# A mixture-of-experts layer on one core: the further block moved behind gate_up, the general test moved to expert 29

## The chip, the cores and the metric

The kernel runs on one core of a Trainium2 chip. The metric is the device time of one execution in microseconds (us), the median of several runs. A profiled execution has a span, from its first to its last instruction, and a little around it that counts in the time but not in the span.

## What is computed

One layer over 256 tokens of width 1024. A first part (modulated norm, four mixers, output projection) ends in a hidden state. Then every token goes to 4 of 32 experts, with softmax gates, and the result is added to the stream and normed:

```
def expert_block(args):
    xb, e = args
    gu = xb @ w_gu[e] + b_gu[e]
    gt = jnp.minimum(gu[:, :D_FF], SWIGLU_LIMIT)
    up = jnp.clip(gu[:, D_FF:], -SWIGLU_LIMIT, SWIGLU_LIMIT)
    act = (up + 1) * (gt * jax.nn.sigmoid(SWIGLU_ALPHA * gt))
    return act @ w_down[e] + b_down[e]
...
x = x + g2 * moe(h_x.reshape(-1, D), *moe_p).reshape(bn, L, D)
return rmsnorm(x, final_norm_g)
```

All weights are float32: 8 MB of gate/up and 4 MB of down weights for each expert, some 400 MB in all. Each is used once, unless an expert has more tokens than fit a block.

## The kernel before

The first part takes some 170 us; the rest is a loop over the experts, in an order written out by hand (each engine runs its instructions in the order of the program; waits between engines are set automatically, as counts of finished work of the engine waited for).

**The ring of weights.** `stream` lists the 192 loads: six for an expert, four of gate/up weights (u = 0 to 3, two of the eight k-slices each) and two of down weights (u = 4, 5), 2 MB each; at the end the last down half of expert 30 stands behind the gate/up loads of expert 31, and the very last load is cut in two. `load_unit(i, e, u)` (lines 566 to 584) puts load i into ring place i mod 9 (`NPAIR`) and notes in `wt` and `dn` where the products find it. `load_to(n)` issues all loads up to n, on SP's queue. Load i must wait until the last instruction that reads load i-9 is done. In the body of expert e, `load_to(e * NUN + NPAIR)` stands behind `down(e - 1)` and issues the loads whose places expert e-1 has used.

**An expert.** The tokens of expert e (the first 64, `CAP`) have been picked one step before. `gate_up(e, XET)` (line 964) multiplies them by the gate/up weights into two banks, four matmuls for each k-slice, so sixteen for each load as the trace counts them. Beside that run `pick` (the next expert's tokens), `swiglu` on VectorE and ScalarE, the transposes `turn_rows` and `turn_act`, and parts of the scatter of the pair of experts before (`adds`: one for an odd expert, three for an even one). `down(e, ...)` (line 992) is the second product; in the program it stands at the beginning of the next expert's body. `keep` moves its result out.

**Further blocks.** If expert e (0 to 29) has over 64 tokens, `block(e, CAP, ...)` (line 1033) computes 32 more with the same weights, both products of them. It is under `tc.If(r > CAP)` on TensorE, VectorE and ScalarE (line 1114), behind `down(e - 1)` and ahead of `gate_up(e)`. `r` is read from the table of counts (`CNT`). On the branch not taken each of these engines does one step that raises its count by what the block would have added.

**The general path** (lines 1149 to 1165) is for inputs in which an expert has still more tokens, or one of the last two over 64. It loads weights again, six loads for each expert, and runs as many blocks as are wanted. Its test is on these engines and SP, behind `gate_up(31)`, in the middle of `down(30)`: four k-slices of `down(30)` stand ahead of `gate_up(31)` and four behind the test. It is not taken for this input.

**The end.** Behind it stand the second half of `down(30)`, `turn_act(AT2)`, and the down product of expert 31 in pieces (`down_half`, line 1011), the last scatter (line 1026) and the final norm.

Of the kernel before, what the change touches and what calls it, by code (L numbers as in the profile page):

```python
# [11 lines left out]
ENG = mybir.EngineType  # L12
# [4 lines left out]
L = 256  # L17
KT = D // P
NE = 32
TOPK = 4  # L20
EPS = 1e-6
CAP = 64
MORE = 32
SLOT = 2048
NSLOT = 18
NUN = 6
NPAIR = NSLOT // 2
# [17 lines left out]

M0 = NSLOT * SLOT
O_ID, O_IOTA, O_POSM, O_GATE, O_VEC = M0, M0 + 128, M0 + 384, M0 + 448, M0 + 512
O_FGB, O_G2B, O_H = M0 + 768, M0 + 1792, M0 + 2304
O_XE, O_XET, O_P, O_PG, O_S = M0 + 4352, M0 + 4864, M0 + 5376, M0 + 5888, M0 + 6144
O_GH, O_TH, O_UP, O_AT, O_O = M0 + 6656, M0 + 7168, M0 + 7680, M0 + 8192, M0 + 8704  # L50
# [19 lines left out]
def tile_hybrid_moe(tc, x, ctx, vec, mats, const, pos_col, pos_row, rows, bias, w_mod, w_in, w_out,  # L70
                    w_gu, w_down, out):
    nc = tc.nc
    pe, dve, act, pool, sp = nc.tensor, nc.vector, nc.scalar, nc.gpsimd, nc.sync

    with tc.tile_pool(name="big", bufs=1) as big, tc.tile_pool(name="acc", bufs=1, space=PSUM) as acc_pool, \
# [7 lines left out]
        CNT = big.tile([1, NE + 1], I32, name="CNT")  # L83
        bank = [acc_pool.tile([P, 512], F32, name=f"bank{i}") for i in range(8)]

        def R(off, n):
            return B[:, off:off + n]

        def slot(i):
            return R(i * SLOT, SLOT)  # L90

# [14 lines left out]
        YT = slot(17).rearrange("p (k n) -> p k n", k=KT)  # L106
        UT = R(14 * SLOT, 4096).rearrange("p (k n) -> p k n", k=KT)
        W_1 = R(8 * SLOT, 8 * 768).rearrange("p (k n) -> p k n", k=KT)
        W_2 = R(11 * SLOT, 8 * 768).rearrange("p (k n) -> p k n", k=KT)
        BMR = R(O_BM, 2048)  # L110
# [357 lines left out]

        sets = [[R(i * SLOT + 512 * j, 512) for j in range(4)] for i in (4, 5, 6, 7)]
        order = [(0, 0), (1, 0), (0, 1), (1, 1)]  # L470
# [88 lines left out]
        wt, dn = {}, {}  # L559
# [3 lines left out]
        stream = [(e, u) for e in range(NE - 2) for u in range(NUN)]  # L563
        stream += [(NE - 2, u) for u in range(5)] + [(NE - 1, u) for u in range(4)] + [(NE - 2, 5), (NE - 1, 4), (NE - 1, 5)]

        def load_unit(i, e, u):

            s = R(2 * RING[i % NPAIR] * SLOT, 2 * SLOT)
            if u < 4:

                sp.dma_start(s, w_gu[e, 256 * u:256 * u + 256, :].rearrange("(p k) n -> p (k n)", k=2))
                for b in range(2):
                    wt[e, 2 * u + b] = s[:, 2048 * b:2048 * b + 2048]
            else:

                h = u - 4
                rows4 = w_down[e, 512 * h:512 * h + 512, :].rearrange("(p k) n -> p k n", k=4)

                step = 2 if (e, u) == (NE - 1, NUN - 1) else 4
                for b in range(0, 4, step):  # L580
                    sp.dma_start(s[:, 1024 * b:1024 * (b + step)].rearrange("p (k n) -> p k n", k=step), rows4[:, b:b + step, :])
                for b in range(4):
                    for q in range(2):
                        dn[e, 4 * h + b, q] = s[:, 1024 * b + 512 * q:1024 * b + 512 * q + 512]

        def load_to(n):
            while nxt[0] < min(n, NE * NUN):
                e, u = stream[nxt[0]]
                load_unit(nxt[0], e, u)
                nxt[0] += 1  # L590
# [307 lines left out]
        GH, TH, UP = R(O_GH, 512), R(O_TH, 512), R(O_UP, 512)  # L898
# [7 lines left out]
        G0, G1 = bank[4], bank[5]  # L906
        mis = [bank[0], bank[1]]
# [7 lines left out]
        def gated(pr):  # L915
            p = PP[pr % 2]
            e0 = 2 * pr
            dve.tensor_tensor(out=PGf.rearrange("p (c e s) -> p c e s", c=2, e=2), in0=p,
                              in1=GT[:, :, e0:e0 + 2].unsqueeze(3).to_broadcast([P, 2, 2, CAP]), op=ALU.mult)
# [40 lines left out]
        def bias_mm(dst, e, col, g):  # L960
            pe.matmul(dst[64 * g:64 * g + 64, :], E3[:, e:e + 1].to_broadcast([96, CAP]), T[:, col:col + 512],  # L961
                      start=True, stop=False)

        def gate_up(e, xt):
            for b, dst in enumerate((G0, G1)):
                for g in range(2):
                    bias_mm(dst, e, b * 1024 + g * 512, g)
            for k in range(KT):
                w = wt[e, k]
                for b, dst in enumerate((G0, G1)):  # L970
                    for g in range(2):
                        pe.matmul(dst[64 * g:64 * g + 64, :], xt[:, k % 4, (k // 4) * 64:(k // 4) * 64 + 64],  # L972
                                  w[:, b * 1024 + g * 512:b * 1024 + g * 512 + 512], start=False, stop=(k == KT - 1))
# [18 lines left out]
        def down(e, dst, ks=range(KT)):  # L992
            for g in range(2):
                if ks[0] == 0:
                    bias_mm(dst, e, 2048 + g * 512, g)
            for k in ks:
                for g in range(2):
                    pe.matmul(dst[64 * g:64 * g + 64, :], AT[:, k % 4, (k // 4) * 64:(k // 4) * 64 + 64],  # L998
                              dn[e, k, g], start=False, stop=(k == KT - 1))
# [20 lines left out]
        def keep(dst, p0, ps):  # L1020
            for g in range(2):
                dve.tensor_tensor(out=dst[p0:p0 + 64, 512 * g:512 * g + 512], in0=ps[64 * g:64 * g + 64, :],  # L1022
                                  in1=G2B[64 * g:64 * g + 64, :], op=ALU.mult)

        def scatter_part(s, o, c, q, a=0, b=512, last=False):
            pe.matmul(Y[c][q][:, a:b], s[:, c * P:(c + 1) * P], o[:, 512 * q + a:512 * q + b], start=False, stop=last)  # L1026
# [6 lines left out]
        def block(e, base, ga, gb, gh, th, up):  # L1033

            n = MORE
            quarter = [slice(n * g, n * g + n) for g in range(4)]
# [46 lines left out]
        engines = [ENG.PE, ENG.DVE, ENG.Activation]  # L1083
# [8 lines left out]
        dve.tensor_reduce(out=cl, in_=CN[0:1, NE - 2:NE], op=ALU.max, axis=mybir.AxisListType.X)  # L1092
        dve.tensor_scalar(cm, cl, float(MORE), cm, op0=ALU.add, op1=ALU.max)
        dve.tensor_copy(CNT[:, NE:NE + 1], cm)
# [6 lines left out]
        pool.memset(VPG, 0.0)  # L1101
        pool.memset(VO, 0.0)
        load_to(NPAIR)

        parts = [(0, 0), (0, 1), (1, 0), (1, 1)]
        for e in range(NE - 1):
            pr, par = divmod(e, 2)
            if e < NE - 2:
                r = nc.values_load(CNT[0:1, e:e + 1], min_val=0, max_val=L, engines=engines)
            if e > 0:  # L1110
                down(e - 1, mis[1])
                load_to(e * NUN + NPAIR)
            if e < NE - 2:
                with tc.If(r > CAP):  # L1114
                    block(e, CAP, G0, G1, GH, TH, UP)
            if e > 0:
                keep(OP[(e - 1) // 2 % 2], 64 * ((e - 1) % 2), mis[1])
            mine = parts if e == NE - 2 else parts[3:] if par else parts[:3]
            adds = [lambda c=c, q=q: scatter_part(SS[(pr - 1) % 2], OP[(pr - 1) % 2], c, q) for c, q in mine]
            adds = adds if pr > 0 else []  # L1120
            gate_up(e, XET)
            if e == NE - 2:
                load_to(NE * NUN)
            pick(PP[(e + 1) // 2 % 2][:, :, (e + 1) % 2, :])

            swiglu()
            picked()
            for f in adds[:1]:
                f()
            turn_rows(XET, mis[1])  # L1130
            turn_act(AT)
            for f in adds[1:]:
                f()
            if par == 1:
                s_pair(PGf, SS[(pr + 1) % 2], G1)
            elif e == 0:
                gated(0)
                s_pair(PGf, SS[0], G1)
            if par == 0 and e + 2 < NE:
                one_hot(pr + 1)  # L1140
                gated(pr + 1)
        e = NE - 1
        more = engines + [ENG.SP]
        r = nc.values_load(CNT[0:1, NE:NE + 1], min_val=0, max_val=L + MORE, engines=more)
        down(e - 1, mis[1], range(4))
        gate_up(e, XET)
        swiglu()

        with tc.If(r > CAP + MORE):  # L1149
            kept = dict(wt), dict(dn)  # L1150
            for e in range(NE):
                base = CAP if e >= NE - 2 else CAP + MORE
                r = nc.values_load(CNT[0:1, e:e + 1], min_val=0, max_val=L, engines=more)
                with tc.If(r > base):
                    for u in range(NUN):
                        load_unit(3 + u, e, u)
                    for b in range(base, L, MORE):
                        args = e, b, mis[0], mis[0], R(O_O, 512), R(O_O + 512, 512), R(O_XET, 512)
                        if b == base:
                            block(*args)  # L1160
                        else:
                            with tc.If(r > b):
                                block(*args)
            for now, old in zip((wt, dn), kept):
                now.update(old)
        e = NE - 1
        down(e - 1, mis[1], range(4, KT))
        keep(OP[1], 0, mis[1])
# [140 lines left out]
```

## Time and profile before

| | us |
|---|---|
| median of 3 runs | 1111.02 (1110.48 to 1111.2) |
| the profiled execution, its time | 1112.09 |
| its span | 1110.3 |
| TensorE (PE) busy | 1025.7 |
| VectorE (DVE) busy | 305.6 |
| ScalarE (ACT) busy | 128.5 |
| moved by the DMA queues | 445.59 MB, mean 401 GB/s |

The page's slices show the busy share of each engine in 40 equal parts of the span, in tenths; PEclk is the granted clock of TensorE in tenths of full speed; under them stand the mean busy share of the 16 DMA engines and the GB/s that they moved. In the timeline a row is a run of like instructions of one line: its start, how long it lasts, engine and line, what is written from what, how many, and in brackets the idle time ahead of it with what ended it. SPq is SP's queue, whose rows are issues of DMAs, PEld TensorE's weight loads, and a q behind an engine its sequencer.

### The profile page before, as it was taken

The page shows a single profiled execution, that of the slowest core. Times are in us where ns is not written, and L with a number is a line of the kernel's source. Part 1 is how long each engine was busy: PE and PEld are TensorE (multiplying, and loading weights), DVE is VectorE, ACT ScalarE, POOL GpSimd, SP SyncE. Part 2 cuts the span into 40 slices and gives each one's busy share as a digit, 9 for nine tenths or more (in the row PEclk, how much of TensorE's full clock was granted, in tenths as well). Part 3 has the DMA queues.
Part 4 walks back from the last instruction along what each step waited for, and adds up shares of the span by engine and source line. Part 5 has one row for each costly group of instructions (what it writes and reads, how often), then busy time and mean ns, then how long its engine had stood idle before and what let it go on. Part 6 is the DMA issues. An engine that isn't in the chain of part 4 may idle for free. (4 is left out here: it accounts for less than half of the span.)

```text
span 1110.3 us, 11952 instructions
## 1 busy us (share of the span) xinstructions
PE 1025.7 (92%) x4932; PEld 435.8 (39%) x4932; DVE 305.6 (28%) x593; ACT 128.5 (12%) x239; POOL 34.6 (3%) x77
## 2 busy tenths in 40 slices
PE   4999988999999989999999999999989898988896
PEld 2665865333333333333333333333333333323333
DVE  5488742121212222121212121212111212111113
ACT  4133430000000000000000000000000000000002
POOL 4102120000000000000000000000000000000000
PEclk8999998999999989999999999999999999999998
DMA  9997888999999998999999999999999999999992
GB/s 298 375 358 314 338 380 333 403 426 426 426 428 424 426 415 357 428 426 427 426 426 426 425 429 425 427 426 426 429 427 424 427 427 428 424 427 427 427 422 119
DMA packets 42098, 445.59 MB, mean 401 GB/s; under 512 B 4676, under 2 KB 6660, under 8 KB 15240
## 3 DMA queue, kind: packets, MB, share of 16 engines
q1 hardware_dynamic: 41352, 443.43, 95.5%
q8 instruction: 80, 1.31, 0.5%
q0 software_dynamic: 640, 0.63, 0.2%
q14 instruction: 26, 0.21, 0.0%
HBM read 442.41 MB, written 1.05 MB: 399 GB/s over the span
## 5 line engine op out<-in xcount | busy, mean ns | idle before, releaser
L972 PE MATMUL bank<-B 128*64 128x512 f32 x2048 | 457.7, 600 | 19.3 <-DMA B<-in_w_gu_dram 18.9
L972 PEld LDWEIGHTS bank<-B 128*64 128x64 f32 x2048 | 167.3, 138 | 290.8 <-issue 242.1
L998 PE MATMUL bank<-B 128*64 128x512 f32 x992 | 222.1, 600 | 2.8 <-PEq L1149 2.8
L976 DVE TENSOR_SCALAR B<-bank 128x512 f32<-128x512 f32 x32 | 22.1, 692 | 455.7 <-issue 403.3
L998 PEld LDWEIGHTS bank<-B 128*64 128x64 f32 x992 | 70.2, 138 | 135.1 <-issue 129.6
L977 ACT ACTIVATE B<-B 128x512 f32<-128x512 f32 x32 | 20.2, 631 | 754.1 <-DVE B L976 754.1
L1022 DVE TENSOR_TENSOR B<-bank,B 64x512 f32<-64x512 f32 x62 | 42.7, 689 | 212.1 <-PE bank L998 211.4
L1026 PE MATMUL bank<-B 128*128 128x512 f32 x136 | 69.1, 616 | 1.2 <-DVE B L1079 1.1
L930 PE MATMUL bank<-B 128*64 128x512 f32 x256 | 61.5, 592 | 0.9 <-DVE B L866 0.9
L961 PE MATMUL bank<-T,E 96*64 96x512 bf16 x190 | 33.4, 394 | 25.4 <-PEq L1114 20.6
L384 PE MATMUL bank<-B 128*128 128x256 f32 x160 | 37.2, 387 | 0.0
L1026 PEld LDWEIGHTS bank<-B 128*128 128x128 f32 x136 | 22.2, 190 | 36.2 <-issue 23.0
L961 PEld LDWEIGHTS <-E 96*64 96x64 bf16 x190 | 10.5, 106 | 65.3 <-issue 64.6
L930 PEld LDWEIGHTS bank<-B 128*64 128x64 f32 x256 | 20.7, 137 | 35.1 <-issue 33.4
L384 PEld LDWEIGHTS bank<-B 128*128 128x128 f32 x160 | 31.1, 195 | 8.3 <-issue 4.3
L942 DVE TENSOR_TENSOR B<-bank,B 128x512 f32<-128x512 f32 x32 | 22.1, 692 | 30.2 <-PE bank L939 30.2
L939 PEld LDWEIGHTS bank<-B 128*128 128x128 f32 x128 | 19.9, 202 | 17.1 <-ACT B L934 16.8
L990 ACT ACTIVATE B<-bank 128x512 f32<-128x512 f32 x32 | 19.1, 597 | 51.6 <-PE bank L989 51.6
L978 DVE TENSOR_SCALAR B<-bank 128x512 f32<-128x512 f32 x32 | 22.1, 691 | 5.3 <-PE bank L972 5.2
L934 ACT ACTIVATE B<-bank 128x512 f32<-128x512 f32 x32 | 19.1, 597 | 38.1 <-PE bank L930 38.1
L539 DVE SCALAR_TENSOR_TENSOR B<-B 128x256 f32<-128x256 f32 x58 | 23.2, 478 | 0.0
L980 DVE SCALAR_TENSOR_TENSOR B<-B 128x512 f32<-128x512 f32 x32 | 22.1, 692 | 3.3
(302 smaller groups left out, 558.9 us busy)
## 6 DMA issues: line engine op xcount, KB each, us to landing
B<-in_w_gu_dram SPq DMA_DIRECT2D x128, 2048.0 KB, 25.9
B<-in_w_down_dram SPq DMA_DIRECT2D x63, 2048.0 KB, 28.8
B<-in_w_mod_dram SPq DMA_DIRECT2D x16, 1024.0 KB, 6.6
B<-in_w_mod_dram SPq DMA_DIRECT2D x16, 512.0 KB, 10.5
B<-in_w_out_dram SPq DMA_DIRECT2D x4, 1024.0 KB
B<-in_w_in_dram SPq DMA_DIRECT2D x8, 384.0 KB, 6.7
B<-in_w_in_dram SPq DMA_DIRECT2D x8, 256.0 KB, 5.1
B<-in_w_down_dram SPq DMA_DIRECT2D x2, 1024.0 KB
```

The costliest lines, as they stand in the source:

```text
L384: pe.matmul(half(b, t), w, UT[:, k, 256:512], start=(k == 0 and t == 0), stop=(k == KT - 1 and t == 1))
L539: dve.scalar_tensor_tensor(dst, src, w, dst, op0=ALU.mult, op1=ALU.add)
L930: pe.matmul(mis[0][64 * g:64 * g + 64, :], p[:, c, :], H[:, c, 512 * g:512 * g + 512], start=(c == 0), stop=(c == 1))
L942: dve.tensor_tensor(out=d4, in0=ps.rearrange("p (j g s) -> p j g s", j=4, g=2), in1=jg(A2s).unsqueeze(3).to_broadcast([P, 4, 2, CAP]), op= ...
L961: pe.matmul(dst[64 * g:64 * g + 64, :], E3[:, e:e + 1].to_broadcast([96, CAP]), T[:, col:col + 512], start=True, stop=False)
L972: pe.matmul(dst[64 * g:64 * g + 64, :], xt[:, k % 4, (k // 4) * 64:(k // 4) * 64 + 64], w[:, b * 1024 + g * 512:b * 1024 + g * 512 + 512], ...
L976: dve.tensor_scalar(GH, G0, 7.0, 0.5, op0=ALU.min, op1=ALU.mult)
L978: dve.tensor_scalar(UP, G1, 7.0, -7.0, op0=ALU.min, op1=ALU.max)
L980: dve.scalar_tensor_tensor(UP, TH, 1.0, UP, op0=ALU.add, op1=ALU.mult)
L998: pe.matmul(dst[64 * g:64 * g + 64, :], AT[:, k % 4, (k // 4) * 64:(k // 4) * 64 + 64], dn[e, k, g], start=False, stop=(k == KT - 1))
L1022: dve.tensor_tensor(out=dst[p0:p0 + 64, 512 * g:512 * g + 512], in0=ps[64 * g:64 * g + 64, :], in1=G2B[64 * g:64 * g + 64, :], op=ALU.mult)
L1026: pe.matmul(Y[c][q][:, a:b], s[:, c * P:(c + 1) * P], o[:, 512 * q + a:512 * q + b], start=False, stop=last)
```

## The change

Two things move. The test and block of expert e go from ahead of `gate_up(e)` to the end of its body, so between its two products; the count for it is read a little earlier or, for expert 0, later. The general path becomes a function that is called once, in the body of expert 29 behind `load_to`; it loads into the places of the six loads issued last (177 to 182), and at its end loads these six again. Its blocks work in the banks and tiles of the ordinary block instead of ones chosen for the tail.

```
+GENERAL = NE - 3
...
+        more = engines + [ENG.SP]
+
+        def general(at):
+            first = at * NUN + NPAIR - NUN
+            r = nc.values_load(CNT[0:1, NE:NE + 1], min_val=0, max_val=L + MORE, engines=more)
+            with tc.If(r > CAP + MORE):
+                kept = dict(wt), dict(dn)
+                for e in range(NE):
+                    base = CAP if e >= NE - 2 else CAP + MORE
+                    r = nc.values_load(CNT[0:1, e:e + 1], min_val=0, max_val=L, engines=more)
+                    with tc.If(r > base):
+                        for u in range(NUN):
+                            load_unit(first + u, e, u)
+                        for b in range(base, L, MORE):
+                            if b == base:
+                                block(e, b, G0, G1, GH, TH, UP)
+                            else:
+                                with tc.If(r > b):
+                                    block(e, b, G0, G1, GH, TH, UP)
+                for i in range(first, first + NUN):
+                    load_unit(i, *stream[i])
+                for now, old in zip((wt, dn), kept):
+                    now.update(old)
...
         for e in range(NE - 1):
             pr, par = divmod(e, 2)
-            if e < NE - 2:
-                r = nc.values_load(CNT[0:1, e:e + 1], min_val=0, max_val=L, engines=engines)
+            count = lambda: nc.values_load(CNT[0:1, e:e + 1], min_val=0, max_val=L, engines=engines)
+            if 0 < e < NE - 2:
+                r = count()
             if e > 0:
                 down(e - 1, mis[1])
                 load_to(e * NUN + NPAIR)
-            if e < NE - 2:
-                with tc.If(r > CAP):
-                    block(e, CAP, G0, G1, GH, TH, UP)
+            if e == GENERAL:
+                general(e)
             if e > 0:
                 keep(OP[(e - 1) // 2 % 2], 64 * ((e - 1) % 2), mis[1])
...
             gate_up(e, XET)
+            if e == 0:
+                r = count()
...
             if par == 0 and e + 2 < NE:
                 one_hot(pr + 1)
                 gated(pr + 1)
+
+            if e < NE - 2:
+                with tc.If(r > CAP):
+                    block(e, CAP, G0, G1, GH, TH, UP)
         e = NE - 1
-        more = engines + [ENG.SP]
-        r = nc.values_load(CNT[0:1, NE:NE + 1], min_val=0, max_val=L + MORE, engines=more)
         down(e - 1, mis[1], range(4))
         gate_up(e, XET)
         swiglu()
-
-        with tc.If(r > CAP + MORE):
...
         e = NE - 1
         down(e - 1, mis[1], range(4, KT))
```

## Rows read from the trace of the kernel before

**Rows 1.** The page: the span, and GB/s in its 40 slices.

```profile
span 1110.3 us, 11952 instructions
...
GB/s 298 375 358 314 338 380 333 403 426 426 426 428 424 426 415 357 428 426 427 426 426 426 425 429 425 427 426 426 429 427 424 427 427 428 424 427 427 427 422 119
```

**Rows 2.** Timeline at expert 0: start us, us, engine, line, what, count, idle before.

```profile
168.11 8.20 SPq L571 DMA_DIRECT2D B<-in_w_gu_dram  x2
170.21 0.62 PE L961 MATMUL bank<-T,E 96*64 96x512 bf16 x3 [1.45 <-issue]
191.98 0.64 PE L961 MATMUL bank<-T,E 96*64 96x512 bf16 x2 [0.30 <-issue]
```

**Rows 3.** Windows: busy time of each engine, then clock, DMA share, GB/s.

```profile
170.00:180.00 10.00, 9.79 (x40) 5.96 (x42) 0.00 (x0) 0.00 (x0) 0.00 (x0) 0.83 0.77 283
180.00:210.00 30.00, 27.50 (x128) 12.28 (x126) 6.62 (x11) 2.21 (x4) 0.00 (x0) 0.94 0.97 403
414.00:424.00 10.00, 10.00 (x46) 3.32 (x46) 0.15 (x1) 0.00 (x0) 0.00 (x0) 1.00 0.56 198
```

**Rows 4.** The line of the gate/up loads, from issue to landing.

```profile
DMA to landing us min/median/max: 7.8/25.9/40.4
```

**Rows 5.** Timeline of experts 8 (with its block) and 9.

```profile
389.92 1.07 PE L1042 MATMUL bank<-B 128*32 128x256 f32 x16
393.11 7.07 PE L1057 MATMUL bank<-B 128*32 128x512 f32 x64 [0.72 <-DVE B L1050]
415.57 0.62 PE L961 MATMUL bank<-T,E 96*64 96x512 bf16 x4
416.03 13.90 PE L972 MATMUL bank<-B 128*64 128x512 f32 x64
419.67 0.33 SPq L571 DMA_DIRECT2D B<-in_w_gu_dram  x1
433.00 0.65 PE L989 MATMUL bank<-B 128*128 128x128 f32 x4
435.30 0.41 PE L961 MATMUL bank<-T,E 96*64 96x512 bf16 x2
443.17 13.93 PE L972 MATMUL bank<-B 128*64 128x512 f32 x64
460.17 0.65 PE L989 MATMUL bank<-B 128*128 128x128 f32 x4
461.12 0.41 PE L961 MATMUL bank<-T,E 96*64 96x512 bf16 x2
```

**Rows 6.** The line of the block's test: TensorE's branch, and who waited for it.

```profile
L1114 PEldq COMPARE_BRANCH  x31: 82/2394/6435, 166.8 to 1006.1; - x31
...
  PE bank L961: 20.9, 28
```

**Rows 7.** Timeline of TensorE, experts 29 to 31.

```profile
1024.96 3.65 PE L972 MATMUL bank<-B 128*64 128x512 f32 x16 [1.23 <-DMA B<-in_w_gu_dram]
1044.54 3.65 PE L972 MATMUL bank<-B 128*64 128x512 f32 x16 [0.55 <-DMA B<-in_w_gu_dram]
1054.32 3.65 PE L972 MATMUL bank<-B 128*64 128x512 f32 x16 [1.24 <-DMA B<-in_w_gu_dram]
1068.32 14.12 PE L972 MATMUL bank<-B 128*64 128x512 f32 x64
...
1085.21 5.35 PE L998 MATMUL bank<-B 128*64 128x512 f32 x16 [2.78 <-PEq L1149]
...
1093.87 5.35 PE L1011 MATMUL bank<-B 128*64 128x256 f32 x48
```

**Rows 8.** The general test: SP's steps, and a weight load it released.

```profile
L1149 SPq EVENT_SEMAPHORE  x8: 17/17/17, 1065.6 to 1091.3; - x8
...
1078.78 0.20 PEld L972 LDWEIGHTS bank<-B 128*64 128x64 f32 x4 [0.88 <-SPq L1149]
```

**Rows 9.** Window of the second half of down(30).

```profile
1085.00:1090.00 5.00, 4.79 (x16) 1.76 (x16) 0.00 (x0) 0.00 (x0) 0.00 (x0) 0.66 0.53 218
```

More of the change, by code (lines that the diff above doesn't have):

```diff
@@ L1147, in tile_hybrid_moe @@
         swiglu()
-        with tc.If(r > CAP + MORE):
[L1150 to L1165, printed above, removed]
         e = NE - 1
```

## The prediction

> **What bounds the kernel now.** I read the page first (span, the busy rows by slices), then the windows, then the timeline of TensorE and of SP's queue, and last the two branches by their source lines. The slices [rows 1] show a stream of weights: from the eighth slice on the DMA engines are full at about 426 GB/s, but for one dip to 357 in the sixteenth, where the one further block of this input runs. Number the loads 0 to 191 in the order of `stream`: six for each expert (four gate/up pairs 6e to 6e+3, two down halves 6e+4 and 6e+5; at the end 185 to 188 are expert 31's pairs, 189 is the last half of expert 30, 190 and 191 are expert 31's). Load n goes into ring place n mod 9, so it waits for the last reader of load n-9. TensorE needs 27.1 us for an expert (416.03 to 443.17 [rows 5]); six loads take 6 x 4.9 = 29.4 us (TensorE gets pairs at 1044.54 and, two loads on, at 1054.32 [rows 7]). TensorE begins late and catches up on the stream; at the end it waits for data, and after the last pair, at 1082.4, a tail of TensorE and VectorE work ends the run [rows 7]. So three things set the time: gaps in the stream, TensorE standing still while data is there, and the tail.
>
> **Change 1: the block behind gate_up, its test with it.** In the program a load waits for a count of TensorE's finished work, and a branch that is not taken raises that count by what the block would have added. Before, the block reads the gate/up weights ahead of gate_up, so gate_up is their last reader and each pair frees its place as it is used. After, the block stands behind gate_up and is the last reader, taken or not: the four places of a pair come free only when TensorE has passed the test. That hits four of six loads of every expert. What it costs depends on how much is still queued then.
>
> *Start.* Load 9 waits on the first quarter of gate_up(0): SP issues it at 168.11 + 8.20 - 0.33 = 176.0 [rows 2], it can land 7.8 us later (the shortest issue to landing [rows 4]), at 183.8. Nothing is queued behind load 8: the DMA share is already 0.77 from 170 to 180 [rows 3]. After, it waits for the test of expert 0, where down(0) begins now, 191.98 [rows 2], and 1.5 us for the branch (below): 193.5, landing 201.3. That is 17.5 us. From 180 to 210 before moved 403 of 426 GB/s [rows 3], a loss of 30 x 5.4% = 1.6 us that the later stream covers: **+16 us** of stream. The test of expert 0 no longer stands before gate_up(0), where TensorE stood 1.45 us [rows 2]; I count no gain, since that fetch comes back at the new place (bounds: 0 to 1.8 us earlier).
>
> *Block of expert 8.* It takes 389.92 to 415.57, 25.65 us, and its gate/up reads end 10.2 us after its start (393.11 + 7.07) [rows 5]. Before, the stream ran dry: from 414 to 424 it moved 198 of 426 GB/s [rows 3], 5.3 us lost, until the first quarter of gate_up(8) freed a place (load 57 at 419.67 [rows 5]). Load 56 was in at about 419.5, so load 51, the last pair of expert 8, at 395; after, 395 + 16 = 411. TensorE waits for it, ends gate_up(8) at 415, begins the block 5.4 us later (an even expert, from 429.9 to 435.30 [rows 5]), at 420.4, and ends its gate/up reads at 430.6, the block at 446.1; down(8) and the start of the next gate_up take 7.9 us (435.30 to 443.17). Loads 57 to 60 go out at 430.6, in time: 56 lands at 435.5, 60 at 455.1, 61 and 62 (freed by down(8)) by 464.9. But load 63 waits for the test of expert 9: gate_up(9) 454.0 to 467.9, 4.0 us to the test (457.1 to 461.12 [rows 5]), 2.5 us branch, 474.4, landing 482.2 instead of 464.9 + 4.9 = 469.8. So 12.4 us are lost where 5.3 were: **+7 us**. The stream is then 23 us late. Later experts have slack: TensorE waits for data, five loads (24.5 us) are queued when gate_up ends and the test comes 4 to 11 us later.
>
> *The branch itself.* On TensorE's queue it took 82 to 6435 ns, median 2394 [rows 6]. Before, 7 us of down matmuls are queued ahead of it, and only 20.9 us in 28 cases showed. After, only what follows the last wait of the step is ahead: 0.9 us for an odd expert (460.17 to 461.1), 2.3 us for an even one (433.00 to 435.30) [rows 5]. Shortest, median and longest expose 0, 1.5 and 5.5 us (odd), 0, 0.1 and 4.1 us (even): I take 2.5 and 1.5 us; the ends stay for the range. Over most experts this is hidden: 27.1 - 0.7 + 2 is still under 29.4. Without that cover it would be some 2 us for each of 29 experts. [...]
>
> **Change 2: the general test at expert 29.** `more` has SP in it. Before, SP comes to this test when every load is out. Its row [rows 8] shows eight semaphore steps from 1065.6 to 1091.3: SP waits for loads in flight to land, semaphore after semaphore, and only then raises each one's count. No load stands behind it there. After, SP comes to it behind load 182, and loads 183 to 191 stand behind it. And as the general path now reloads the places of loads 177 to 182, the readers of these loads must wait for counts that SP raises in the branch not taken. The loads go over eight semaphores in turn; in the program's order (semaphore 0 first) SP waits for loads 179, 180 and 181 before it raises the count that gate_up(29) needs for load 177. So the last quarter of gate_up(29) waits for load 181.
>
> Before, load 177 came at 1024.96, 181 at 1044.54 [rows 7]. After: 1044.5 + 23 = 1067.5, with SP's steps 1067.8; the quarter would have begun at 1048: TensorE stands about 20 us. Then nothing hides it: quarter 3.65 us, plus 1.7 for the clock (after the 2.8 us stop at 1085.21 sixteen matmuls took 5.35 for 3.65, granted 0.66 of full speed, some at 1.2 GHz [rows 7, 9]): 1073.2; 4.0 to the test and 2.5 branch, as at expert 9: 1079.7; 7.9 for down(29) and the start of gate_up(30): 1087.6; 13.9 for it: 1101.5; 10.35 to gate_up(31) (1057.97 to 1068.32), which takes 14.1: 1126.0, against 1082.44 [rows 7]: **+43.6 us** with the 23 in it. Load 183 goes out at 1079.6, after 182 is in (1072.4): the stream stops again, but 183 lands at 1087.4 and 188 at 1111.9, each ahead of its reader. The engines' own tests there cost nothing: they lie in the 20 us. POOL takes no part.
>
> **Change 3: the tail without its test.** Now TensorE ends gate_up(31) at 1082.44, stands 2.8 us and runs 5.35 us to 1090.56 [rows 7]; after, 3.65 us at once: **-4.4 us** (load 189 is in at 1116.8). With the loads as they are now it would be little smaller: SP's last step there, a landing, is at 1091.3 [rows 8].
>
> Sum: 1110.3 + 43.6 - 4.4 = 1149.5 us of span. Around the span lie 1112.09 - 1110.3 = 1.8 us, and the median, 1111.02, is 1.07 under the profiled run: **1150 us**.
>
> **Rivals.** *One, SP holds only itself.* If the counts are raised in an order that frees load 177 first, or its reader keeps the old count, TensorE is not stopped, and load 183 goes out before 182 lands: 23 us remain, less part of the tail: gate_up(31) ends at 1105.5, down(30) at 1110.4, the quarters of expert 31 by 1119.2, 11.1 us more as now (1099.2 [rows 7] to 1110.3): 1130.3 of span, 1131. For it: loads 175 to 178 are long in. Against it: the program's order, and that a TensorE weight load at 1078.78 is released by SP's branch [rows 8].
> *Two, faster.* The places come free as early as now, or enough is queued to cover the delay. It decides at load 9: if SP still issues it by about 177, no stream is lost, the block's dry 5.3 us go, and the tail gains 4.3: 1110.3 - 9.6 + 0.7 = 1101. Against it: the share of 0.77 when load 9 is issued; the queue is empty there.
> *Three, short branches.* Were every branch as short as the shortest, 82 ns, because its target is always fetched in time, 1.5, 2.5 and 2.5 us fall away: 1144. Against it: the median of 2394 ns [rows 6]. [...]
> *Four, worse:* SP waits for 182 too (+4.9) and expert 29's branch is the longest (+3.1): 1158.
> That the general path would run I leave out: the trace shows its not-taken steps.
>
> **How the numbers follow.** Forecast 0.54, one 0.20, two 0.07, three 0.10, four 0.09. The range goes from under rival one, 1128, to four, 1158; it leaves out two and part of four. Faster by over 0.2% (about what this measurement can tell from no change) is two, 0.07; 0.03 lies between, where a small loss of stream cancels against the tail; slower 0.90.
>
> **What would show it.** Start: SP's first load after gate_up(0) at 192 to 196 instead of 176, a hole in the DMA row from 177 on. Block: loads of expert 10 late, a hole of some 10 us after it. Branch: idle before L998's bias matmul instead of before gate_up's. General: some 20 us before the last sixteen matmuls of gate_up(29), released by SP's branch. Tail: no stop after gate_up(31). The prediction fails if load 9 is on time, or if that stop is missing.

## The result, and the profile after

| | before | after |
|---|---|---|
| median of 3 runs, us | 1111.02 (1110.48 to 1111.2) | 1153.33 (1151.63 to 1153.61) |
| the profiled execution, its time | 1112.09 | 1153.33 |
| its span | 1110.3 | 1151.5 |
| mean granted clock of TensorE | 0.978 | 0.957 |

The ratio after to before is 1.0378, 95% interval 1.0354 to 1.0401. The forecast was 1150, slower. So the sum was right to 3 us, but one of its two large terms came about in another way than the text says.

The page of after (span, GB/s in 40 slices of 28.8 us; beside [rows 1]):

```profile
span 1151.5 us, 11953 instructions
...
GB/s 302 382 345 322 363 306 206 427 368 428 425 427 427 426 424 386 256 426 425 421 428 427 427 425 427 418 425 427 394 426 416 427 409 427 426 426 423 256 430 122
```

Three large holes are to be seen: 206 in the seventh slice (load 9), 386 and 256 in the sixteenth and seventeenth (the block), 256 in the thirty-eighth (the general test). The same holes by windows (columns as in [rows 3]: busy time of the five engines, clock, DMA share, GB/s):

```profile
170.00:180.00 10.00, 10.00 (x50) 3.23 (x47) 0.00 (x0) 0.00 (x0) 0.00 (x0) 1.00 0.52 197
180.00:190.00 10.00, 6.99 (x38) 2.98 (x35) 5.24 (x9) 2.21 (x4) 0.00 (x0) 0.97 0.07 16
...
460.00:470.00 10.00, 10.00 (x50) 3.33 (x48) 1.00 (x2) 0.44 (x1) 0.00 (x0) 1.00 0.37 156
...
1060.00:1070.00 10.00, 1.31 (x7) 0.17 (x3) 0.00 (x0) 0.00 (x0) 0.00 (x0) 0.83 1.01 428
```

In the last of these windows the DMA engines are full and TensorE does nothing from 1061.3 on: it waits for SP. The timeline of after, expert 0 (beside [rows 2]), the loads behind the block, and TensorE from expert 29 on (beside [rows 7]):

```profile
168.91 20.21 SPq L572 DMA_DIRECT2D B<-in_w_gu_dram  x2
169.26 13.90 PE L973 MATMUL bank<-B 128*64 128x512 f32 x64
189.56 0.64 PE L962 MATMUL bank<-T,E 96*64 96x512 bf16 x2 [0.90 <-PEq L1175]
...
433.93 40.04 SPq L572 DMA_DIRECT2D B<-in_w_gu_dram  x4
...
1050.39 0.62 PE L962 MATMUL bank<-T,E 96*64 96x512 bf16 x4 [2.57 <-PEq L1114]
1050.82 10.49 PE L973 MATMUL bank<-B 128*64 128x512 f32 x48
1072.77 5.71 PE L973 MATMUL bank<-B 128*64 128x512 f32 x16 [11.46 <-SPq L1114]
1090.24 13.90 PE L973 MATMUL bank<-B 128*64 128x512 f32 x64
1114.48 13.90 PE L973 MATMUL bank<-B 128*64 128x512 f32 x64
1128.22 3.60 PE L999 MATMUL bank<-B 128*64 128x512 f32 x16
```

What TensorE waited for (us in total, times, longest), and what the test's branch took (beside [rows 6]):

```profile
PE bank L962 <- PEq L1175: 43.2, 11, 6.0
PE bank L962 <- DVEq L1175: 15.9, 18, 0.9
PE bank L973 <- SPq L1114: 11.5, 1, 11.5
```

```profile
L1175 PEldq COMPARE_BRANCH  x31: 70/345/6478, 188.2 to 1080.9; - x31
...
  PE bank L962: 59.1, 29
```

No wait of L973 (gate_up) on a load of weights stands in this view of after. Before there were 19 such waits, 18.9 us:

```profile
PE bank L972 <- DMA B<-in_w_gu_dram: 18.9, 19, 2.6
```

So in after TensorE waited for the late stream only once, through SP (the 11.5 us). It was late itself, by 59.1 us of stops at the tests where before showed 20.9 [rows 6]. Three of these stops, with the down matmuls behind two of them:

```profile
502.16 0.41 PE L962 MATMUL bank<-T,E 96*64 96x512 bf16 x2 [0.88 <-DVEq L1175]
502.40 7.04 PE L999 MATMUL bank<-B 128*64 128x512 f32 x32
...
532.82 0.64 PE L962 MATMUL bank<-T,E 96*64 96x512 bf16 x2 [5.27 <-PEq L1175]
533.24 9.22 PE L999 MATMUL bank<-B 128*64 128x512 f32 x32
...
562.95 0.41 PE L962 MATMUL bank<-T,E 96*64 96x512 bf16 x2 [0.88 <-DVEq L1175]
```

There are two kinds: 18 of 0.9 us and 8 of 3.8 to 6.0 us; three more lie between 0.15 and 1.95. A short stop is not the branch itself. Ahead of 502.16 the branch began at 498.3 and took 0.31 us, and TensorE worked on until 501.28. Only then come its step of the branch not taken and, right behind it, the read of the next expert's count (line 1137), with nothing queued on TensorE:

```profile
L1175 PEldq EVENT_SEMAPHORE  x1: 51/51/51, 501.3 to 501.3; - x1
L1137 PEldq TENSOR_LOAD <-CNT x1: 306/306/306, 501.5 to 501.5; - x1
```

The waits put these stops down to VectorE's step (DVEq), which came at 501.4, ahead of the read. Behind the test of expert 29 no count is read, and there the stop is 0.15 us (in e3 below as well). By that a read right behind a test costs some 0.73 us, some 20 of the 59.1 us (an estimate, 28 x 0.73). In before no test stands right ahead of the read, and no stop shows at it.

Behind a long stop the same 32 matmuls of down take 9.22 us instead of 7.04, at a mean granted clock of 0.67 from 533 to 540 us (0.50 to 537, 1.00 from 538 on; behind the short stop it is 1.00):

```profile
533.00:540.00 7.00, 7.00 (x24) 2.25 (x24) 0.00 (x0) 0.00 (x0) 0.00 (x0) 0.67 1.01 414
563.00:570.00 7.00, 7.00 (x34) 2.47 (x36) 0.00 (x0) 0.00 (x0) 0.00 (x0) 1.00 0.98 405
```

### The profile page after: what moved, and what is told of

It reads as the page before. It is cut to its first block, busy times and chain, and to the rows that moved or that the text cites. A ratio compares the mean times of both kernels' runs of the same rounds, so it can differ in the third digit from the quotient of the medians.

```text
span 1151.5 us, 11953 instructions
## 1 busy us (share of the span) xinstructions
PE 1032.5 (90%) x4932; PEld 436.2 (38%) x4932; DVE 305.4 (27%) x593; ACT 128.3 (11%) x239; POOL 34.5 (3%) x77
## 3 DMA queue, kind: packets, MB, share of 16 engines
q8 instruction: 80, 1.31, 0.5%
## 5 line engine op out<-in xcount | busy, mean ns | idle before, releaser
L973 PE MATMUL bank<-B 128*64 128x512 f32 x2048 | 450.4, 594 | 11.5 <-SPq L1114 11.5
L973 PEld LDWEIGHTS bank<-B 128*64 128x64 f32 x2048 | 157.0, 137 | 285.2 <-issue 262.6
L999 PE MATMUL bank<-B 128*64 128x512 f32 x992 | 244.6, 642 | 5.8 <-issue 5.8
L962 PE MATMUL bank<-T,E 96*64 96x512 bf16 x190 | 36.9, 408 | 64.1 <-PEq L1175 43.2
L931 PE MATMUL bank<-B 128*64 128x512 f32 x256 | 65.2, 606 | 0.9 <-DVE B L867 0.9
```

The costliest lines, as they stand in the source:

```text
L931: pe.matmul(mis[0][64 * g:64 * g + 64, :], p[:, c, :], H[:, c, 512 * g:512 * g + 512], start=(c == 0), stop=(c == 1))
```

## The experiments

Two theories on change 1. **S, the stream:** the gate/up places come free late, loads go out late, TensorE waits for them (the recorded text). **B, the branches:** the tests stop TensorE itself, now that little is queued ahead of them. On change 2: SP in the branch not taken frees the count for load 177 only when load 181 is in (the recorded text), or not. The kernel before ran beside them: its median was 1108.73 us at the first four kernels below, 1108.79 at the next four, 1108.45 at the last three, and the ratios are to its runs there.

### Each change alone

*e1_block_alone*: the kernel after with the general path put back behind `gate_up(31)`.

```
             if e > 0:
                 down(e - 1, mis[1])
                 load_to(e * NUN + NPAIR)
-            if e == GENERAL:
-                general(e)
...
+        with tc.If(r > CAP + MORE):
...
```

> Change 1 alone: test and block of an expert stand behind gate_up as in the kernel after; the general test stays behind gate_up(31) as before. Taken from the trace of after: there gate_up(29) starts at 1050.82 us, 37.8 later than before, and what change 2 adds behind it is a stop of 11.46, some 2.1 of slower clock in the quarter behind it and a branch of some 2.6. Without these, and with the old tail (4.7 longer), the span is 1151.5 - 16.2 + 4.7 = 1140, the time about 1141. Both theories give this number: S (the stream is late because the places come free late) and B (TensorE itself is made slower by the branches, with nothing queued ahead to hide them). If the two changes don't add up, it lies elsewhere: 1131 would be the 23 us that the prediction counted for change 1 (1111 + 23 = 1134, less some of the tail).

Measured: 1141.46 us (1135.15 to 1142.43), ratio to before 1.0279, interval 1.0242 to 1.0316. Change 1 costs 32.7 us by itself.

*e2_general_alone*: the kernel after with an expert's test and block ahead of gate_up again.

```
             if e == GENERAL:
                 general(e)
+            if e < NE - 2:
+                with tc.If(r > CAP):
+                    block(e, CAP, G0, G1, GH, TH, UP)
...
-            if e < NE - 2:
-                with tc.If(r > CAP):
-                    block(e, CAP, G0, G1, GH, TH, UP)
```

> Change 2 alone: the general path in the body of expert 29, the test and block of an expert ahead of gate_up as before. Theory: TensorE can't begin the last quarter of gate_up(29) before load 181 is in, 1044.54 by the trace of before, instead of 1024.96: a stop of some 19.5 us, longer than the 11.46 in the trace of after, where TensorE itself was late. The loads behind 182 go out late as well, and part of the stop is given back, since TensorE waited for data in the last experts anyway: gate_up(31) ends some 14 us later, the tail gains 4.4: about 1120. Rival (SP holds only itself, as rival one of the prediction): no stop, 1107 to 1111.

Measured: 1122.82 us (1121.97 to 1123.72), ratio 1.0125, interval 1.0107 to 1.0143: change 2 costs 14.1 us. The parts add up to 46.8; both together cost 42.3. TensorE at expert 29 in e2:

```profile
1017.04 1.07 PE L962 MATMUL bank<-T,E 96*64 96x512 bf16 x4 [10.24 <-PEq L1145]
1017.87 12.75 PE L973 MATMUL bank<-B 128*64 128x512 f32 x48
1042.20 5.68 PE L973 MATMUL bank<-B 128*64 128x512 f32 x16 [11.58 <-SPq L1114]
```

The stop at the last quarter ends about where it was expected (1042.20, expected 1044.54), but it is 11.58 us and not 19.5: TensorE came to it late, since it had stood 10.24 us ahead of gate_up(29), where two branches stand one behind the other. That piece was not expected.

### Hold or branch

*e3_block_reads_down*: e1, but the block reads other places.

```
             pe.matmul(ga[quarter[g], :], VXT[:, k % 2, n * (k // 2):n * (k // 2) + n],
-                      wt[e, k][:, 512 * g:512 * g + 512], start=False, stop=(k == KT - 1))
+                      dn[e, k, g % 2], start=False, stop=(k == KT - 1))
```

> As e1, but the block takes its gate/up weights from the places of the down weights, so that it no longer reads a gate/up place and these come free in gate_up, as before; the branch stays behind gate_up. (It leaves out the right weights in the one block that runs.) It parts the hold of the places from the branch. S (late stream): the loads go out as before, load 9 at about 176 us, and the time is that of before, about 1111. B (branches on TensorE): nothing changes for TensorE, which still takes some 29.9 us for an expert: about 1141. A mixture lies between, and what it gains on e1 is the price of the hold.

Measured: 1139.8 us (1138.68 to 1143.1), ratio 1.0284, interval 1.0259 to 1.0309. Load 9 is early again (169.04 + 4.33 - 0.33 = 173.0 us), the stream is full there (426 GB/s from 180 to 210), and the time is that of e1:

```profile
169.04 4.33 SPq L571 DMA_DIRECT2D B<-in_w_gu_dram  x2
```

```profile
PE bank L961 <- PEq L1144: 45.0, 10, 5.8
PE bank L961 <- DVEq L1144: 16.0, 18, 0.9
```

TensorE's stops are those of after. With these stops in the way, the hold of the places is worth 1.7 us, less than the two can be told apart.

*e4_hold_no_tests* and *e5_no_hold_no_tests*: no tests of the experts; e5 has `H[:, 0, P * u:P * u + P]` in place of the weights.

```
-            if e < NE - 2:
-                with tc.If(r > CAP):
-                    block(e, CAP, G0, G1, GH, TH, UP)
+            if e == 8:
+                block(e, CAP, G0, G1, GH, TH, UP)
+            elif e < NE - 2:
+                for u in range(4):
+                    pe.transpose(G0[:, P * u:P * u + P], wt[e, 2 * u + 1][:, 0:P], ident)
```

> The other half: no test of an expert at all (the block runs for expert 8 unconditionally, behind gate_up), but at the end of each expert's body four transposes on TensorE read the four gate/up places, so that these are held as long as in e1; the general test is where it was before. (It leaves out the tests of the other experts.) S: the stream stands at load 9 until about 190 and after the block as in after: some 22 us late, 1111 + 22 = 1133. B: TensorE has no branch left and catches up on what is there: 1108, not over 1113.

> The control of e4: the same kernel without the tests of the experts, the block of expert 8 unconditional and behind gate_up, the same four transposes on TensorE, but they read the hidden state instead of the four gate/up places, so that these come free in gate_up. (It leaves out the tests of the other experts.) Only the block still holds its places. e5 against e4 is the price of the hold when no branch stands in the way. Theory B (the time of after is TensorE's own, the hold costs only where TensorE is not late anyway): 1106 to 1110, so e4 lies some 10 above it, although e1 and e3 lie together. Rival (the hold costs nothing in either): as e4, 1119.

Measured: e4 1119.69 us (1117.42 to 1122.16), ratio 1.0096, interval 1.0071 to 1.0121; e5 1096.69 us (1094.92 to 1098.68), ratio 0.9892, interval 0.987 to 0.9915. Both expectations of e4 and the figure for e5 missed, because they started from the time of before. That time has 30 tests in it and a stream that runs dry twice; e5 has neither and is 12 us less. How much of the 12 belongs to which is not shown. GB/s moved in four stretches of the span, and what that loses against 426:

| | 170 to 230 us | 230 to 400 | 400 to 500 | 500 to 1000 | lost, us |
|---|---|---|---|---|---|
| before | 392 | 426 | 404 | 426 | 10.0 |
| after | 314 | 417 | 365 | 422 | 38.4 |
| e3 | 402 | 414 | 358 | 424 | 26.5 |
| e4 | 320 | 428 | 385 | 428 | 24.6 |
| e5 | 427 | 428 | 426 | 428 | 0 |

The difference e4 - e5 is 23.0 us of time and 24.6 of stream: the price of the hold where no test stands in the way. That it is also the forecast's 16 + 7 is chance. The forecast counts from before, and against before the stream of e4 lost 10.1 us more at the start and 4.5 at the block. With the first runs this makes a table of the two causes:

| us | places free in gate_up | places held to the end of the body |
|---|---|---|
| no tests | e5 1096.69 | e4 1119.69 |
| tests behind gate_up | e3 1139.8 | e1 1141.46 |

The hold costs 23.0 without tests and 1.7 with them; the tests cost 43.1 without the hold and 21.8 with it. They don't add up: the later of the two decides, and in after that is TensorE. (e4 and e5 also have four small transposes an expert that e1 and e3 have not.) A late TensorE holds up the stream as well: e3, whose places are free in gate_up, loses 26.5 us of it. The waits for weights agree (TensorE in e4, then in e5):

```profile
L972 PE MATMUL bank<-B 128*64 128x512 f32 x2048 | 456.7, 595 | 51.3 <-DMA B<-in_w_gu_dram 51.3
```

```profile
L972 PE MATMUL bank<-B 128*64 128x512 f32 x2048 | 452.7, 594 | 33.9 <-DMA B<-in_w_gu_dram 33.0 <-SPq L1150 0.8
```

*e9_half_the_tests*: e3 with `if e < NE - 2 and e % 2 == 0` at the count and at the test.

> As e3 (places not held by the block), but with a test for the even experts only. (It leaves out the tests of the odd experts, and the right weights in the one block.) It tells whether branch and stream add up or whether the longer one alone counts. By the larger of the two: TensorE takes 27.1 + 29.9 us for two experts, 28.5 for one, less than the stream's 29.4, and has caught up by the end: 169.4 + 31 x 28.5 + 13.9 + 27.9 = 1095 of span, near the 1092.8 of e5, so 1096 to 1101. By the sum: half of what e3 lies above e5 (1139.8 - 1096.7 = 43), so 1118.

Measured: 1104.08 us (1101.09 to 1106.75), ratio 0.9961, interval 0.9944 to 0.9977: 3 us over the band for the larger of the two, 14 under the sum. Half the tests take away 35.7 of 43.1 us. But the run doesn't part the two theories as it was meant to. TensorE's stops at the tests fall from 61.0 us to 13.8 (four of 3.1 to 3.9), not to half: no count is read right behind these tests, and the short stops are gone with it. A sum in proportion to the stops gives 1096.7 + 43.1 x 13.8 / 61.0 = 1106, as near as the larger of the two. What parts the theories is the table above. TensorE catches up in e9 and waits for weights 22 times, 22.0 us in all; in e3 it never does:

```profile
PE bank L972 <- DMA B<-in_w_gu_dram: 22.0, 22, 1.2
```

### Cover

*e6_block_after_down*: test and block of expert e-1 behind `down(e - 1)`. *e10_block_straight*: test and block of expert e straight behind its `gate_up`, in the bank of down.

```
             if e > 0:
                 down(e - 1, mis[1])
+                with tc.If(r > CAP):
+                    block(e - 1, CAP, G0, G1, GH, TH, UP)
                 load_to(e * NUN + NPAIR)
```

```
             gate_up(e, XET)
+            if e < NE - 2:
+                with tc.If(r > CAP):
+                    block(e, CAP, mis[1], mis[1], GH, TH, UP)
```

> The test and block of expert e-1 stand behind down(e-1) in the body of expert e (general test as before): 7 us of down matmuls are queued ahead of the branch, as in the kernel before, but the places of the pair are held still longer, down to the end of down. It parts cover from hold the other way round. B (branches without cover on TensorE): the stops before L961 fall to the 20.9 us of before, and 1141 falls to about 1120, where the longer hold decides (1118 to 1128). S (hold): as e1 or worse, 1141 to 1150.

> Test and block of an expert straight behind its gate_up, ahead of pick and swiglu (the block in the bank of down instead of gate_up's two, general test as before). The branch has the 14 us of gate_up queued ahead of it on TensorE, and the places are held only to the end of gate_up, some 4 us less than in e1. If the stops in after are branches without work queued ahead, they are gone here, below the 20.9 us of before, and what is left is the hold: load 9 at about 184 us (188 in e4), a little less than e4, 1112 to 1118. If the stops don't depend on what is queued ahead: as e1, 1135 to 1141.

Measured: e6 1141.67 us (1141.0 to 1142.15), ratio 1.029, interval 1.0267 to 1.0312; e10 1118.51 us (1115.24 to 1119.66), ratio 1.009, interval 1.0061 to 1.0119. In e6:

```profile
PE bank L972 <- DMA B<-in_w_gu_dram: 44.6, 44, 1.6
PE bank L961 <- PEq L1112: 23.9, 28, 2.4
```

With 7 us of down ahead of the branch, and no read of a count right behind it, the stops fall from 61 to 23.9 us and none is over 2.4: B is right on the cover, but not on the time. But the places are held through down as well (load 9 at 165.97 + 29.64 - 0.33 = 195.3), and now the stream is the later one: TensorE waits 44.6 us for weights, and the time is that of e1 by the other cause. In e10, with 14 us ahead:

```profile
PE bank L930 <- PEq L1120: 28.0, 28, 3.0
```

No stop is over 3.0 us here either, but 28.0 us are left, not less than with 7 us ahead, and the time is just over the band: that expectation missed. The trace shows why. In before (from expert 1 on) and in e6 TensorE's queue comes to the branch 4.4 us before its last matmul ends, and in e10, with twice as much queued, 3.6 to 4.4 us before. A branch of 0.3 us is hidden by that, and 0.2 to 0.3 us of stop are left; nine branches in e10 take 5.8 to 6.5 us and leave 1.7 to 3.0 each:

```profile
L1120 PEldq COMPARE_BRANCH  x1: 6323/6323/6323, 230.9 to 230.9; - x1
```

```profile
225.70 9.61 PE L972 MATMUL bank<-B 128*64 128x512 f32 x44
237.51 1.94 PE L930 MATMUL bank<-B 128*64 128x512 f32 x8 [2.20 <-PEq L1120]
```

The matmuls end at 235.31 and the branch at 237.2. In after the queue comes to the branch only some 1.5 us ahead (odd experts) or 2.7 to 3.0 (even, from expert 2 on).

### The general test

*e7_after_turned* is after, *e8_general_turned* is e2, each with four small loads more, which turn the order of the loads over the semaphores:

```
         load_mod(12)
         load_out(2)
+        for g in range(4):
+            sp.dma_start(SPARE[:, 32 * g:32 * g + 32], const[:, 32 * g:32 * g + 32])
```

> The kernel after, with four small loads of constants more in the first part. They do nothing but turn the order in which the loads go over the eight semaphores by four, so that the count that gate_up(29) wants for load 177 is raised first in SP's row of steps, when load 175 is in, instead of behind those for loads 179 to 181. Theory of the recorded prediction: the stop of 11.46 us and the slow quarter behind it are gone, 1153.3 - 11.5 - 2 = 1140, about 1139 to 1142. Rival (SP or the other engines hold TensorE in another way): 1153.

> Change 2 alone as in e2, with the four small loads of e7. No stop at gate_up(29); the general test is gone from the tail (some 4.4 us); SP stands in the branch until load 181 is in, 1044.5 us, and only then issues load 183, about when 182 is in. By the theory of the prediction 1107, some 4 us under before and 15 under e2; by a rival (SP's own hold empties the queue, so that every later load is some 3 to 8 us late) 1111 to 1116.

Measured: e7 1141.73 us (1135.86 to 1143.26), 11.6 under after. The stop of TensorE is gone, though SP still takes its steps as late; what is left ahead of gate_up(29) is the branch:

```profile
L1117 SPq EVENT_SEMAPHORE  x8: 17/17/17, 1057.9 to 1074.9; - x8
```

```profile
1053.87 0.62 PE L965 MATMUL bank<-T,E 96*64 96x512 bf16 x4 [2.64 <-PEq L1117]
1054.30 13.93 PE L976 MATMUL bank<-B 128*64 128x512 f32 x64
```

So the stop was the order in which SP raises the counts, as the forecast has it. e8: 1109.71 us (1107.44 to 1112.25), ratio 1.0004, interval 0.9992 to 1.0017: no change, between the two numbers expected. The shorter tail is there, and is spent at the two branches one behind the other; from there to the end of gate_up(31) TensorE waits for no load:

```profile
1019.52 1.07 PE L965 MATMUL bank<-T,E 96*64 96x512 bf16 x4 [10.21 <-PEq L1148]
...
1072.56 13.90 PE L976 MATMUL bank<-B 128*64 128x512 f32 x64
```

gate_up(31) begins 4.2 us later than the 1068.32 of before [rows 7], and the tail is some 4 shorter.

*e11_general_at_30*: e8 with `GENERAL = NE - 2` and six small loads instead of four.

> As e8, but the general path in the body of expert 30, which has no test of its own, with six small loads ahead so that the count for load 183 is raised first. In e8 TensorE stands 10.2 us ahead of gate_up(29) at two branches one behind the other, and SP's hold opens a gap ahead of load 183. Here one branch stands behind down(29), SP has only loads 189 to 191 left, and its hold ends with the landing of load 187, some 1074 us. If these two ate the gain of e8, the 4.4 us of the tail come out: 1104 to 1106 against some 1109. If the hold of SP still costs what the tail gains: 1109.

Measured: 1106.61 us (1105.18 to 1108.16), ratio 0.9978, interval 0.9964 to 0.9992. It beats both kernels, by 0.2% against before: 1.8 us of the 4.4 hoped for, just over the band. One branch is left ahead of gate_up(30), 2.74 us, gate_up(31) begins as before, and down(30) follows it at once:

```profile
1040.64 0.62 PE L965 MATMUL bank<-T,E 96*64 96x512 bf16 x4 [2.74 <-PEq L1117]
...
1067.94 13.90 PE L976 MATMUL bank<-B 128*64 128x512 f32 x64
1081.97 3.65 PE L1002 MATMUL bank<-B 128*64 128x512 f32 x16
```

## Why the prediction was right, and where it was not

*Start: mechanism right, size too large.* SP issued load 9 at 168.91 + 20.21 - 0.33 = 188.8, not 193.5. The test of expert 0 no longer stands ahead of gate_up(0), which began at 169.26 and ran 13.90 us for 15.81; the text counted no gain there and gave 0 to 1.8 us as bounds; with the faster run it ended 3.1 us earlier (183.16 for 186.26). That the 1.45 us before are a fetch, as the text has it, was its estimate: the one packet of the queue of instructions (q8) near them began at 167.9 us, and the stop at 168.8. The stream lost 11.0 us more there than before (314 against 392 GB/s from 170 to 230), forecast 16.

*Block: the time right, the way not.* Load 63 went out at 433.93 + 40.04 - 0.33 = 473.6, forecast 474.4. But the forecast has TensorE wait for load 51 until 411. It waited for no load: gate_up(8) began at 403.1, late by the stops ahead of it, and ran through. The stream lost 9.2 us more than before (365 against 404 GB/s from 400 to 500), forecast 7.

*"The stream is then 23 us late" and "TensorE waits for data": the first right, the second wrong.* By 500 us the stream of after had lost 23.7 us more than that of before, by 1000 us 28.4 (the table of stretches). But apart from the stop at SP TensorE waited for no weights, and e3, with load 9 on time, is no faster than e1.

*"Over most experts this is hidden: 27.1 - 0.7 + 2 is still under 29.4": this step failed.* The mean stop was sized well: 59.1 us in 29 is 2.04 us a test, forecast 1.5 and 2.5. That is luck in part, for the forecast made it of TensorE's branch alone, with a median of 2394 ns. In after the median is 345 ns, and some 20 of the 59.1 us are the reads of the next count, a term that the forecast did not have. Two other terms were not sized well. First, 27.1 us is one expert behind a short branch. The mean of before is more: from the first bias matmul of gate_up(9), 0.43 ahead of 443.17 [rows 5], to that of gate_up(18) it is 247.27 us, 27.5 for each of nine:

```profile
690.01 0.62 PE L961 MATMUL bank<-T,E 96*64 96x512 bf16 x4 [0.16 <-PEq L1114]
```

Second, the slower clock behind a long stop was priced at expert 29 alone. Down's matmuls in all, before and then after:

```profile
L998 PE MATMUL bank<-B 128*64 128x512 f32 x992 | 222.1, 600 | 2.8 <-PEq L1149 2.8
```

```profile
L999 PE MATMUL bank<-B 128*64 128x512 f32 x992 | 244.6, 642 | 5.8 <-issue 5.8
```

That is 22.5 us more, and 5.8 of idle time among them that names no other engine. So 27.5 + (59.1 - 20.9 + 22.5 + 5.8) / 29 = 29.8, an estimate that leaves out lines which became up to 7 us faster or slower, and 29.8 is what the trace shows (gate_up(9) begins at 455.69, gate_up(29) at 1050.82: 595.13 us for 20 experts, with the 2.57 us at the general test in them). That is over 29.4. And the comparison itself was not enough: TensorE starts behind a full ring, so its pace must be well under 29.4 to catch up before the end. Before, at 27.5, first waits for weights at 781 us; e9 goes at 27.1 (gate_up(9) begins at 435.82, gate_up(18) at 679.96) and first waits at 772.

*General: right, at another time.* The third quarter of gate_up(29) ended at 1050.82 + 10.49 = 1061.3, not at the forecast 1048, so the stop was 11.46 us, not 20; its end is set by the load that SP waits for, forecast 1067.8 by SP's steps, measured 1072.8. The slow quarter took 5.71 us (forecast 3.65 + 1.7), at a mean granted clock of 0.64. No run shows the 1.2 GHz that stands beside the 1.7; the trace of before shows a granted share of 0.50 there, from 1086 to 1089 us. e7 shows the cause of the stop.

*Tail: right.* From the end of gate_up(31) to the end of the span: 1151.5 - 1128.4 = 23.1 us; before 1110.3 - 1082.44 = 27.9. That is -4.8, forecast -4.4.

Why the sum came out all the same is luck in part. TensorE came to the last quarter of gate_up(29) 13.3 us later than forecast, late by its own stops and not by waiting for the stream. The stop there was 8.3 us shorter for it, since it ends with a landing, and load 181 was there 28.2 us later than before (1072.77 against 1044.54), forecast 23. Of the 5.0 us that were left, the way to the end of gate_up(31) gave 2.6 back (1128.4, forecast 1126.0). Rival one (no stop) gave 1131: without the stop it was 1141.73, so its 23 us are too few in the same way. Rival three (short branches) fell with the stops of up to 6.0 us. That a branch is short where its target is fetched in time agrees with the trace of before: each of TensorE's 18 branches of over 2.1 us at these tests overlaps a packet on the queue of instructions (q8), and none of the 13 of up to 0.37 us does. Its 82 ns, the shortest branch, was that of expert 8, whose block runs; a branch past a block took 318 ns at the least in before and 313 in after.

## What to carry to other kernels

Two delays on two engines that feed each other through a ring did not add up here: the tests alone cost 43.1 us, the hold alone 23.0, both 44.8 (e3, e4 and e1 against e5). So compare which is later. And the engine that started behind had not caught up by expert 29 at 29.8 us an expert against the stream's 29.4 (after); at 27.5 it first waited for weights at 781 us (before): its pace must be clearly under the other's before its own stops are hidden. A conditional block that is not run cost by what its engine has queued ahead of the branch (61 us in e3, 24 in e6, and no less, 28, in e10 with more queued), by a read that stands right behind it (some 0.73 us, an estimate from the stops of 0.88 and 0.15) and by what the block holds (23 us in e4); moving it is a trade between these. Before an engine that issues loads is put under a test, look at which counts it raises in the branch not taken, in what order, and what it must see landed first: in after that was a stop of 11.46 us, gone in e7 with another order.

## What was not expected of the hardware

The stops at the tests are of two kinds, and the long ones mostly come three experts apart (experts 5, 11, 14, 17, then 18, 21, 24 and 27, behind which TensorE restarts at 339.88, 532.82, 620.46, 708.46, 740.75, 832.56, 923.37 and 1010.15 us). During a long stop the trace shows one packet on the queue of instructions (the DMA queues from 527.5 to 532.9; packets, MB, share):

```profile
q1 hardware_dynamic: 155, 2.28, 99.5%
q8 instruction: 1, 0.02, 1.2%
```

All nine of TensorE's branches of over 3.9 us at these tests in after have one such packet within them, and none of the 22 shorter ones has. Over the whole span this queue moved 80 packets, 1.31 MB, in after (80 in before too) and 42, 0.69 MB, in e5, which has no tests of the experts: 16 KB a packet. Where a test fails, the program jumps past its block, so a long branch may be one that waits for the instructions behind the block: the packets agree with that in place, but that the branch waits for them is not shown. Their number alone shows less, since the program of e5 is shorter as well. Whether the full weight queue makes the transfer slow is not shown: no run here took the load off it. That TensorE's queue gets no more than 4.4 us ahead of its matmuls at a test, whether 7 or 14 us of them are queued (before, e6 and e10), was not expected either; it is why more cover does not take the rest of the stop away.
